# Softmax over 16384 rows: the first two tiles, of 3 and 5 rows, become one tile of 8 rows

## The chip, the core and the metric

One core of a Trainium2 chip runs the whole kernel. The time is device microseconds (us) of one execution; a kernel is given by the median of its runs. Beside it stands the profile of one execution: its span runs from the first to the last instruction of the program.

## The reference

```python
x = np.random.randn(16, 1024, 512).astype(np.float32)

temp = 2.0
x_scaled = x / temp
x_max = np.max(x_scaled, axis=-1, keepdims=True)
exp_x = np.exp(x_scaled - x_max)
return (exp_x / np.sum(exp_x, axis=-1, keepdims=True)).astype(np.float32)
```

A softmax of 16384 rows of 512 float32 values, 33.55 MB in and 33.55 MB out.

## The kernel before

The 16384 rows are 128 rows for each of the 128 partitions of the on-chip memory (SBUF). From here on "a row" is one row per partition: 128 x 512 values, 256 KB. A tile of r rows takes 128 x r neighbouring rows of the input, and partition p holds r of them that lie next to each other in DRAM. So one tile of 15 rows moves as 128 pieces of 30,720 bytes, and the pitch from one partition's piece to the next is 30,720 bytes too.

Ten tiles (`TILES`, L10) cover the 128 rows: 3, 5, and eight of 15. They lie in an arena of 98 rows; the second number of each entry is its place there. The first eight tiles fill the arena. The last two, 8 and 9, are put where the first ones were: `LATE` (L14) says that tile 8 may be loaded when the stores of tiles 0, 1 and 2 have landed, and tile 9 when that of tile 3 has.

The softmax is taken without the maximum. For each row ScalarE (ACT) computes exp(x/2) in place and sums it into `stats` (L204 for the 3 rows of `HEAD`, L271 for groups of five rows). VectorE (DVE) then takes for each group of the list `pairs` one reciprocal of the sums (L166) and one multiplication over all rows of the group (L169). A group never reaches over a tile's end: one group of 3 rows, one of 5, one of 15 for each further tile, and three of 5 rows in the last tile, which is the one where `most` is 1. At the end the sums are tested (L180 to L190); if one were out of bounds, loops further down would compute everything again with the maximum. With this input they do not run.

The order of the work around the change is written out by hand:

- `early()` puts the loads of tile 0 on SP's DMA queue and that of tile 1 on ACT's, ahead of everything else. Tile 0 is loaded in three parts (`SPREAD`): its first row for 126 partitions, the same row for the other two, then rows 1 and 2 for all.
- `loads()` puts tiles 2 to 7 on ACT's queue right after that. Nothing there waits for anything, since these tiles have places of their own in the arena.
- POOL waits until all rows before row 83 (`TURN`) have gone through ACT, then for the stores that `LATE` names, and issues the loads of tiles 8 and 9 (L119, from L179).
- TensorE's queue waits for each tile's load in turn and adds to the semaphore `s_go` the number of groups that ACT may begin (L194). ACT takes one from it before each group.
- SP issues the stores, one for each tile in order, each when the multiplication of the tile's last group is done (`store`, L135).

So the SP queue holds three loads and ten stores, the ACT queue seven loads, and the POOL queue two.

Of the kernel before, what the change touches and what calls it, by code (L numbers as in the profile page):

```python
# [7 lines left out]


TILES = [  # L10
    (3, 0), (5, 3), (15, 8), (15, 23), (15, 38), (15, 53), (15, 68), (15, 83), (15, 0), (15, 15),
]

LATE = {8: (0, 1, 2), 9: (3,)}  # L14
ARENA = 98

HEAD = [3]
E = 5

SPREAD = 0  # L20

TURN = 83

# [5 lines left out]
def kernel(  # L29
# [5 lines left out]
    nc = tc.nc  # L35
# [9 lines left out]
    P = nc.NUM_PARTITIONS  # L45
# [14 lines left out]
    tiles, base = [], 0  # L60
# [5 lines left out]
    def dram(ap, t):  # L66
        b, r, _ = tiles[t]
        return ap[b * P : (b + r) * P].rearrange("(p r) d -> p r d", r=r)

    def sb(t):  # L70
        _, r, at = tiles[t]
        return arena[:, at : at + r, :]
# [5 lines left out]
    owner = [max(t for t, (b, _, _) in enumerate(tiles) if b <= s) for s in starts]  # L78
# [10 lines left out]
    upto = [1 + max(j for j, ks in enumerate(pairs) if owner[ks[0]] == t) for t in range(len(tiles))]  # L89

    ld = [nc.alloc_semaphore(f"ld{t}") for t in range(len(tiles))]
    s_home = {t: nc.alloc_semaphore(f"s_home{t}") for t in LATE}
    s_near = nc.alloc_semaphore("s_near")
    s_end = nc.alloc_semaphore("s_end")
    s_exp = nc.alloc_semaphore("s_exp")
    s_go = nc.alloc_semaphore("s_go")
# [13 lines left out]
    g_rec = nc.alloc_semaphore("g_rec")  # L110
    g_mul = nc.alloc_semaphore("g_mul")

    def load(eng, t):
        r = tiles[t][1]
        parts = [(0, P, 0, r)]
        if t == SPREAD:
            parts = [(0, 126, 0, 1), (126, P, 0, 1), (0, P, 1, r)]
        for p, q, lo, hi in parts:
            eng.dma_start(  # L119
                out=sb(t)[p:q, lo:hi], in_=dram(xf, t)[p:q, lo:hi]  # L120
            ).then_inc(ld[t], 16)

    stored_by = {u: s_home[t] for t, us in LATE.items() for u in us}
    for t, (_, r, at) in enumerate(tiles):
        over = {u for u, (_, ru, au) in enumerate(tiles[:t]) if at < au + ru and au < at + r}
        assert over <= {u for v, us in LATE.items() if v <= t for u in us}

    def landings(ts):
        return 16 * len(list(ts))
# [21 lines left out]
            eng.reg_add(i, i, 1)  # L151

    def early():
        load(nc.sync, 0)
        load(nc.scalar, 1)

    def loads():
        for t in range(2, min(LATE)):
            load(nc.scalar, t)

    def program():
# [14 lines left out]
        nc.gpsimd.wait_ge(s_exp, starts.index(TURN))  # L176
        for t, us in LATE.items():
            nc.gpsimd.wait_ge(s_home[t], landings(us))
# [11 lines left out]
        )._wait_ge(s_tot, 1).then_inc(s_flag, 1)  # L190


        for t in range(len(tiles)):
            nc.tensor.wait_ge(ld[t], 48 if t == SPREAD else 16).then_inc(s_go, owner.count(t))  # L194
        nc.tensor.wait_ge(s_ones, 1)
        nc.tensor.matmul(  # L196
            total[:, :], lhsT=count[:, :], rhs=ones[:, :], start=True, stop=True
# [83 lines left out]
    entry.instructions = []  # L281
    nc.switch_bb("main", None)
    early()
    first = list(entry.instructions)
    at = next(k for k, i in enumerate(head) if type(i).__name__ == "InstDrain")
    entry.instructions = head[:at] + first + head[at:]
    act = []
    entry.instructions = list(entry.instructions) + [i for i in jumps if i not in act]
    nc.switch_body(here, parent=None, valid_engines=[i.engine for i in jumps])
    loads()  # L290
    program()


# [28 lines left out]
```

## Time and profile before

| | |
|---|---|
| median of 4 runs | 160.06 us (160.0 to 160.12) |
| the profiled execution | 160.1 us |
| its span | 158.8 us |
| DVE busy | 73.2 us of the span |
| ACT busy | 80.4 us |
| TensorE, POOL busy | 0.2 and 2.2 us |
| bytes moved | 67.11 MB, 423 GB/s over the span |
| first exponential, first multiplication | begin at 14.85 and 17.04 us |
| stores of tiles 0 and 1 issued | at 18.82 and 22.97 us |
| last store issued | at 135.68 us |

An engine's busy time leaves out the instructions that issue DMAs and wait for semaphores. The DMA share is that of the core's 16 DMA engines, which all queues feed. Every DMA of the kernel that covers all 128 partitions consists of 128 data packets, one for each partition's piece, and 16 small ones of 4 bytes that report the landing. The trace has a record for each packet with its queue, start, duration and bytes; queue q1 is SP's, q10 ACT's, q0 POOL's.

### The profile page before, as it was taken

Reading aid. Unit: us, or ns where it says so; the run is one execution under the profiler, and the core shown is the slowest. Engines: PE = TensorE matmul, PEld = TensorE weight load, DVE = VectorE, ACT = ScalarE, POOL = GpSimd, SP = SyncE. Lnnn points to the kernel's source line nnn. Section 1 sums busy time; section 2 is a strip of 40 time slices with the busy share of each in tenths; the row PEclk is TensorE's granted clock in tenths of the full one; section 3 lists DMA queues with packets and bytes.
Section 4 is the critical chain, followed back from the end, with each engine's and each line's share of the span. In section 5 each row is a group of like instructions: output and inputs, shape, how many; then the busy total and the mean of one; then the engine's idle time right before and its main releaser. Section 6 shows DMA issues by size and latency. Waiting matters only on the chain. (4 is left out here: it accounts for less than half of the span.)

```text
span 158.8 us, 657 instructions
## 1 busy us (share of the span) xinstructions
PE 0.2 (0%) x2; PEld 0.1 (0%) x2; DVE 73.2 (46%) x27; ACT 80.4 (51%) x257; POOL 2.2 (1%) x8
## 2 busy tenths in 40 slices
PE   0000000000000000000000000000000000000000
PEld 0000000000000000000000000000000000000000
DVE  0000470698979913980079300595199199200000
ACT  0302999999990696009920099459800994000000
POOL 0000000000000000000030000000000001000000
DMA  6998999899898989899999999999999999999995
GB/s 215 479 444 381 472 420 416 382 435 493 364 503 387 480 387 480 387 464 402 464 403 464 403 464 402 457 410 449 418 449 418 449 418 441 426 441 426 433 426 255
DMA packets 3024, 67.11 MB, mean 423 GB/s; under 512 B 336, under 2 KB 336, under 8 KB 720
## 3 DMA queue, kind: packets, MB, share of 16 engines
q1 hardware_dynamic: 1728, 34.34, 50.6%
q10 hardware_dynamic: 1008, 24.90, 36.7%
q0 software_dynamic: 288, 7.86, 11.5%
HBM read 33.55 MB, written 33.55 MB: 423 GB/s over the span
## 5 line engine op out<-in xcount | busy, mean ns | idle before, releaser
L271 ACT ACTIVATE arena<-arena x125 | 76.6, 613 | 38.6 <-ACTq L140 38.6
L169 DVE TENSOR_TENSOR arena<-arena,recip 128x7680 f32<-128x7680 f32 (+2 forms) x12 | 70.2, 5847 | 0.4
L166 DVE RECIPROCAL recip<-stats 128x15 f32<-128x15 f32 (+2 forms) x12 | 2.7, 224 | 62.4 <-ACT arena L271 45.5
L271 ACT ACTIVATION_READ_ACCUMULATOR arena<-arena x125 | 23.3, 186 | 0.0
L204 ACT ACTIVATE arena<-arena 128x512 f32<-128x512 f32 x3 | 1.9, 618 | 8.5 <-ACTq L140 8.5
L200 ACT ACT_TABLE_LOAD x1 | 1.3, 1283 | 5.0 <-issue 5.0
L119 POOL DMA_DIRECT2D arena<-in_x_dram x2 | 1.3, 630 | 79.5 <-ACT arena L271 78.4
L180 POOL TENSOR_SCALAR inside<-stats 128x128 f32<-128x128 f32 x1 | 0.6, 629 | 49.6 <-ACT arena L271 49.6
L204 ACT ACTIVATION_READ_ACCUMULATOR arena<-arena 128x1 f32 x3 | 0.6, 186 | 0.0
L196 PE MATMUL total<-ones,count 128*1 128x1 f32 x2 | 0.2, 164 | 135.9 <-DVE inside L184 135.9
L184 DVE SCALAR_TENSOR_TENSOR inside<-inside,stats 128x128 f32<-128x128 f32 x1 | 0.3, 284 | 0.0
L188 DVE TENSOR_SCALAR flag<-total 1x1 int32<-1x1 f32 x1 | 0.1, 147 | 0.3 <-PE total L196 0.3
L196 PEld LDWEIGHTS total<-ones,count 128*1 128x1 f32 x2 | 0.1, 80 | 135.9 <-DVE inside L184 135.9
L175 POOL MEMSET ones<- 128x1 f32 x1 | 0.1, 98 | 1.7 <-POOLq L37 1.7
L306 POOL MEMSET const-float32-0.0<- 128x1 f32 x1 | 0.1, 104 | 0.2 <-issue 0.2
L306 POOL MEMSET const-bfloat16-1.0<- 128x1 bf16 x1 | 0.1, 107 | 0.0
L306 POOL MEMSET const-uint8-127<- 128x1 uint8 x1 | 0.1, 107 | 0.0
L306 POOL MEMSET const-float32-1.0<- 128x1 f32 x1 | 0.1, 104 | 0.0
L184 DVE DVE_READ_ACCUMULATOR inside<-inside,stats 128x1 f32 x1 | 0.1, 83 | 0.0
## 6 DMA issues: line engine op xcount, KB each, us to landing
out_dram<-arena SPq DMA_DIRECT2D x8, 3840.0 KB, 33.3
arena<-in_x_dram ACTq DMA_DIRECT2D x6, 3840.0 KB, 42.1
arena<-in_x_dram POOLq DMA_DIRECT2D x2, 3840.0 KB, 32.2
arena<-in_x_dram ACTq DMA_DIRECT2D x1, 1280.0 KB, 7.0
out_dram<-arena SPq DMA_DIRECT2D x1, 1280.0 KB, 22.8
out_dram<-arena SPq DMA_DIRECT2D x1, 768.0 KB, 14.8
arena<-in_x_dram SPq DMA_DIRECT2D x1, 512.0 KB
arena<-in_x_dram SPq DMA_DIRECT2D x1, 252.0 KB
```

Of the source, the lines that this page charges most:

```text
L119: eng.dma_start(out=sb(t)[p:q, lo:hi], in_=dram(xf, t)[p:q, lo:hi]).then_inc(ld[t], 16)
L166: nc.vector.reciprocal(out=recip[:, b : b + c], in_=stats[:, b : b + c])._wait_ge(s_exp, ks[-1] + 1).then_inc(s_rec, 1)
L169: nc.vector.tensor_mul(out=arena[:, a : a + c], in0=arena[:, a : a + c], in1=recip[:, b : b + c].unsqueeze(2).to_broadcast([P, c, D]),)._w ...
L175: nc.gpsimd.memset(ones[:, :], 1.0).then_inc(s_ones, 1)
L180: nc.gpsimd.tensor_scalar(out=inside[:, :], in0=stats[:, :], scalar1=LO, scalar2=HI, op0=Alu.max, op1=Alu.min,)._wait_ge(s_exp, len(sizes) ...
L184: nc.vector.scalar_tensor_tensor(out=inside[:, :], in0=inside[:, :], scalar=1.0, in1=stats[:, :], op0=Alu.mult, op1=Alu.is_equal, accum_ou ...
L188: nc.vector.tensor_scalar(out=flag[:, :], in0=total[:, :], scalar1=float(N), scalar2=None, op0=Alu.is_ge,)._wait_ge(s_tot, 1).then_inc(s_f ...
L196: nc.tensor.matmul(total[:, :], lhsT=count[:, :], rhs=ones[:, :], start=True, stop=True)._wait_ge(s_cnt, 2).then_inc(s_tot, 1)
L200: nc.scalar.preload_act_table(Exp)
L204: ins = nc.scalar.activation(out=arena[:, b], in_=arena[:, b], func=Exp, scale=0.5, accum_out=stats[:, b : b + 1],)
L271: ins = nc.scalar.activation(out=data, in_=data, func=Exp, scale=0.5, accum_out=stats[:, r : n_rows - E + 1 + r][:, bass.ds(now, 1)],)
L306: nc = _bacc.Bacc("TRN2", target_bir_lowering=False, num_devices=1)
```

## The change

Tiles 0 and 1 become one tile of 8 rows. Its load is still cut at row 3 and comes by the same four DMAs with the same bytes from the same two queues; the parts up to row 3 report to a semaphore of their own, `ld_first`. As the tile's rows are 8 for each partition, partition p now holds the rows 8p to 8p+7 of the first 1024 rows of the input, where it held the rows 3p to 3p+2 of the first 384 and 5p to 5p+4 of the next 640. In DRAM the pitch from one partition's piece to the next is therefore 16,384 bytes in place of 6,144 and 10,240.

ACT's groups stay 3, 5, 5, ... rows. DVE's groups follow the tiles, so the first is one of 8 rows. There is one store of 8 rows in place of two of 3 and 5. All later tiles keep their rows and their places; their numbers fall by one, and `LATE` with them.

```diff
 TILES = [
-    (3, 0), (5, 3), (15, 8), (15, 23), (15, 38), (15, 53), (15, 68), (15, 83), (15, 0), (15, 15),
+    (8, 0), (15, 8), (15, 23), (15, 38), (15, 53), (15, 68), (15, 83), (15, 0), (15, 15),
 ]

-LATE = {8: (0, 1, 2), 9: (3,)}
+LATE = {7: (0, 1), 8: (2,)}
...
-SPREAD = 0
+FIRST = 3
...
+    ld_first = nc.alloc_semaphore("ld_first")
...
-    def load(eng, t):
-        r = tiles[t][1]
-        parts = [(0, P, 0, r)]
-        if t == SPREAD:
-            parts = [(0, 126, 0, 1), (126, P, 0, 1), (0, P, 1, r)]
-        for p, q, lo, hi in parts:
+    def load(eng, t, parts=None):
+        for sem, p, q, lo, hi in parts or [(ld[t], 0, P, 0, tiles[t][1])]:
             eng.dma_start(
                 out=sb(t)[p:q, lo:hi], in_=dram(xf, t)[p:q, lo:hi]
-            ).then_inc(ld[t], 16)
+            ).then_inc(sem, 16)
...
     def early():
-        load(nc.sync, 0)
-        load(nc.scalar, 1)
+        r = tiles[0][1]
+        load(nc.sync, 0, [
+            (ld_first, 0, 126, 0, 1), (ld_first, 126, P, 0, 1), (ld_first, 0, P, 1, FIRST),
+        ])
+        load(nc.scalar, 0, [(ld[0], 0, P, FIRST, r)])

     def loads():
-        for t in range(2, min(LATE)):
+        for t in range(1, min(LATE)):
             load(nc.scalar, t)
...
-        for t in range(len(tiles)):
-            nc.tensor.wait_ge(ld[t], 48 if t == SPREAD else 16).then_inc(s_go, owner.count(t))
+        nc.tensor.wait_ge(ld_first, 48).then_inc(s_go, 1)
+        nc.tensor.wait_ge(ld[0], 16).then_inc(s_go, owner.count(0) - 1)
+        for t in range(1, len(tiles)):
+            nc.tensor.wait_ge(ld[t], 16).then_inc(s_go, owner.count(t))
```

## The prediction

> **What bounds the kernel now.** I read the page's engines and slices first, then the DMA queues, the DMA by stretches, and who waits for whom.
>
> ```profile
> span 158.8 us, 657 instructions
> PE 0.2 (0%) x2; PEld 0.1 (0%) x2; DVE 73.2 (46%) x27; ACT 80.4 (51%) x257; POOL 2.2 (1%) x8
> ...
> DMA  6998999899898989899999999999999999999995
> ...
> DMA packets 3024, 67.11 MB, mean 423 GB/s; under 512 B 336, under 2 KB 336, under 8 KB 720
> ```
>
> No compute engine is busy for more than 51%, while the DMA engines stand at 8 or 9 tenths in every slice but the first and the last. The stretches (length, PE, PEld, DVE, ACT, POOL, clock, DMA share, GB/s) say the same more finely:
>
> ```profile
> 0.00:4.00 4.00, 0.00 (x0) 0.00 (x0) 0.00 (x0) 0.00 (x0) 0.31 (x5) 1.00 0.67 213
> 4.00:24.00 20.00, 0.00 (x0) 0.00 (x0) 4.95 (x4) 10.43 (x31) 0.00 (x0) 1.00 1.02 436
> 24.00:48.00 24.00, 0.00 (x0) 0.00 (x0) 16.95 (x5) 23.53 (x78) 0.00 (x0) 1.00 1.01 431
> 48.00:84.00 36.00, 0.00 (x0) 0.00 (x0) 20.21 (x6) 18.58 (x60) 1.26 (x2) 1.00 1.01 436
> 84.00:124.00 40.00, 0.00 (x0) 0.00 (x0) 21.71 (x5) 19.30 (x63) 0.00 (x0) 1.00 1.00 431
> 124.00:156.00 32.00, 0.19 (x2) 0.09 (x2) 9.39 (x9) 8.57 (x29) 0.63 (x1) 1.00 1.00 430
> ```
>
> From 4 us to 156 us the share is 1.00 to 1.02. Loads alone (4 to 23 us), loads beside stores, and stores alone (124 us on) all run at 430 to 436 GB/s, so it doesn't matter for the end which queue is served when, as long as one has work. The waits of SP's queue and of POOL (engine line, waited for, total us, times, longest):
>
> ```profile
> SPq L137 <- DVE arena L169: 130.3, 10, 20.2
> SPq L257 <- DMA out_dram<-arena: 22.7, 1, 22.7
> ```
> ```profile
> POOL arena L119 <- ACT arena L271: 78.4, 1, 78.4
> POOL arena L119 <- DMA out_dram<-arena: 1.1, 1, 1.1
> ```
>
> The last store is issued at 135.68 us and SP then waits 22.7 us for bytes: a backlog, not a computation. The chain that ended last (DVE 6%, mostly L169) stops at the flag, at 136 us; it isn't the limit. Span = start of the DMAs + all packets + the end.
>
> **The change part by part.** The sum is made for the profiled execution, 158.8 us of span and 1.3 us around it = 160.1 us, 0.04 us above the median; I carry differences over to the median of 160.06.
>
> *The loads at the start.* SP's three DMAs (126x512, 2x512, 128x1024) and ACT's one (128x2560) stay, as do their queues, their order and their bytes. Nothing is moved past them. What is new is the pitch in DRAM, 16,384 bytes for 6,144 and 10,240. No row shows that pitch. The packet records give what the old ones cost: in the first 7 us the packets take, summed and divided by 16 engines, 0.65 us more than a straight line through the sizes (84 ns at 2 KB, 385 ns at 10 KB, 1138 ns at 30 KB, the medians). Bounds: half of the 0.65 us goes (-0.32), or it doubles (+0.65). The nearest rows are ACT's loads: 393 ns median at the pitch of 10,240 and 1141 at 30,720 in the first tiles, 2% and 0.3% above the line; the pitch matters little there. I take 0.
>
> *A rule that speaks against it.* The Trainium skill ("DMA: Bandwidth & Descriptors", Latency and other measured facts) gives copies of 128 pieces of 16 KiB a lower rate where the pitch between partitions is a large power of two: 207 GB/s at 512 KiB and 103 at 4 MiB, against 214. Ours becomes a power of two, but 16 KiB, and it equals the piece, so the store is contiguous. Its mildest figure, 3% of 4.2 MB, would be an estimated 0.3 us; no run here shows it.
>
> *ACT.* Groups stay 3 and 5 rows; the first begins when row 0 to 2 have landed, as now (14.85 us). Cost 0.
>
> *DVE.* Two reciprocals (0.17 and 0.19 us) and two multiplications (128x1536 in 1.76, 128x2560 in 2.82 us) become one of each. The line through 1.76, 2.82 and 8.16 us for 3, 5 and 15 rows gives 4.42 us for 8, the reciprocal 0.21. DVE now begins when ACT has done row 7, at 19.89 us, and ends at 19.89+0.21+4.42+0.06 = 24.58 us, in place of 22.94. Next on it is the first 15-row group, whose reciprocal begins at 29.07 us, after 6.13 us of idling; 4.5 us of this are left. Hidden: 0. Without that cover 1.6 us of DVE would be late.
>
> *The stores.* Those issued at 18.82 and 22.97 us become one at about 24.6 us. What is queued behind it on SP is the 15-row store at 37.5 us, which waits for DVE anyway. The first store's packets began 4.0 us after its issue (22.84 us) and spread to 32.0 us, since each of its 6 KB packets takes turns with a 30 KB load packet; the second's ran from 33.9 to 44.3 us. The new one begins at 24.6+4.0 = 28.6 us; its 8 packets for each engine take turns with 8 load packets, 8 x (611+1138) ns = 14.0 us, so it ends near 42.6 us. (611 ns: the line above at 16,384 bytes.) From 22.8 to 28.6 us ACT's queue alone feeds the engines; its last load ends at 88.6 us, so it can't run dry, and loads alone already run at full rate. Cost of the delay: 0. The next stores come up to 1.7 us earlier, the loads of this phase correspondingly later, by a microsecond at most.
>
> *What waits for those.* POOL's first late load waited for ACT (the 78.4 us row), and may go a microsecond later than 80.72 us; its packets begin at 85.0 us, while ACT's load queue lasts to 88.6 and SP's backlog throughout. The last store is issued at 135.68 us and its first packet leaves at 148.3: 12.6 us of slack against at most 1 us. Cost 0; with that cover gone it would be 1 us.
>
> *What really leaves the path.* Each engine had 8 packets of 234 ns and 8 of 385 ns for the two stores; now it has 8 of 611: 8 x (619-611) = 0.06 us. One 4-byte report packet for each engine, 9 ns, goes too. Together -0.07 us. SP's second issue (0.33 us) and its wait were under the transfers: 0.
>
> *What I can't price exactly.* Between 20 and 48 us, load packets near the begin of these stores ran up to 1387 in place of 1138 ns; summed and divided by 16 engines the excess is 0.22 us, and there is next to none (0.02) from 48 to 86 us. One store fewer may take a share of it away, or a heavier one add to it. Bounds -0.22 and +0.22; I take -0.03, a small share, as the slow packets stand in three bunches (21.6 to 26, 35.8 to 37.4, 45.0 to 46.4 us), and only one store goes.
>
> *A rule for it.* The same page (Bandwidth, Measured) asks for DMAs of at least 1 MiB; its fit of 2.0 us + bytes/436e3 would price 768 KB and 1280 KB at an estimated 3.8 + 5.0 us and the one of 2048 KB at 6.8, 2.0 us less, which would give 158.1. The trace disagrees for this place: the pause between two stores (32.0 to 33.9 us) is filled by load packets at full rate.
>
> Sum: 160.06 - 0.07 - 0.03 = 159.96 us.
>
> **The rivals.**
>
> - *The front gets dearer.* 16 engines read at once, and with the pitch at 16 KB their addresses lie powers of two apart. For: the first 7 us already carry 0.65 us of slow packets, and lost DMA time is lost for good, since no later stage has slack in the DMA. Against: 393 for 385 ns is all that the pitch of 10,240 costs a median packet. If the 0.65 us doubles, 160.06-0.07+0.65 = 160.64 us, slower. It decides from an extra 0.39 us on (0.32 over the median, plus the 0.07 saved).
> - *The disturbances go.* If the 0.22 us between 20 and 48 us belong to the small stores, and half of the front's excess goes: 160.06-0.07-0.22-0.32 = 159.45 us. For: the bunches lie near the stores' issues at 22.97, 37.55 and 46.73 us. Against: the store at 18.82 has none beside its issue, and two of the three bunches belong to stores that stay.
> - *The late store leaves the engines idle.* The first store comes 5.8 us later; were all of it idle, 160.06+5.8 = 165.9 us. Against: ACT's load queue covers it, with 60 us to go.
> - *The change doesn't do what it says.* The order of instructions shows one store of 128x4096 for two and the loads as before; no chance left for this.
>
> **How the numbers follow.** What a measurement of this kernel can tell from no change is about 0.2%, 0.32 us: 159.74 to 160.38. Chances: the forecast 0.62, the dearer front 0.17, the disturbances gone 0.18, idle engines 0.03. Faster 0.19 (a little of the forecast's own spread added), same 0.61, slower 0.20. The forecast's bounds are 160.06-0.07-0.22 = 159.77 and 160.06-0.07+0.22 = 160.21; the range is drawn half-way towards the two rivals, 159.6 to 160.4.
>
> **What would show it.** After: a DMA share of 1.00 in every stretch from 4 to 156 us; 2880 packets (3024 - 144); one store of 2048 KB issued near 24.6 us and landing near 43.5; a multiplication 128x4096 of 4.4 us; the first exponential near 14.85 us; SP's last wait near 22 us; a span of 158.6 to 158.8 us. Wrong if a stretch after 4 us falls below 1.00, if the first exponential comes more than 0.4 us later, or if the packets of 2, 4 and 10 KB take more than 5% over 84, 159 and 393 ns in the median.

## The result and the profile after

The changed kernel takes 160.23 us (median of 35 runs, 159.93 to 160.91), the one before, run beside it, 159.99 us (56 runs). The ratio is 1.0016, 95% interval 1.0010 to 1.0021: slower by 0.24 us, where 0.10 us less was forecast. It is within the 0.2% that was called no change, and inside the range, but the interval excludes both no change and a gain. The profiled execution took 160.21 us.

The page of the changed kernel, its span, engines, slices and DMA:

```profile
span 158.9 us, 654 instructions
PE 0.2 (0%) x2; PEld 0.1 (0%) x2; DVE 72.9 (46%) x25; ACT 80.4 (51%) x257; POOL 2.2 (1%) x8
...
DMA  7999999899989898989898989898989898989895
...
DMA packets 2880, 67.11 MB, mean 422 GB/s; under 512 B 320, under 2 KB 320, under 8 KB 576
...
out_dram<-arena SPq DMA_DIRECT2D x8, 3840.0 KB, 31.0
...
out_dram<-arena SPq DMA_DIRECT2D x1, 2048.0 KB, 19.2
```

The change did what it says: 144 packets fewer and one store of 2048 KB in place of two. The DMA engines are as full as before. The stretches of the changed kernel (same columns as in the prediction):

```profile
0.00:4.00 4.00, 0.00 (x0) 0.00 (x0) 0.00 (x0) 0.00 (x0) 0.31 (x5) 1.00 0.70 210
4.00:24.00 20.00, 0.00 (x0) 0.00 (x0) 3.16 (x2) 9.52 (x28) 0.00 (x0) 1.00 1.01 433
24.00:48.00 24.00, 0.00 (x0) 0.00 (x0) 18.29 (x5) 23.59 (x77) 0.00 (x0) 1.00 1.02 430
48.00:84.00 36.00, 0.00 (x0) 0.00 (x0) 16.82 (x4) 19.33 (x64) 0.00 (x0) 1.00 0.99 427
84.00:124.00 40.00, 0.00 (x0) 0.00 (x0) 22.60 (x6) 18.69 (x62) 1.27 (x2) 1.00 1.02 439
124.00:156.00 32.00, 0.19 (x2) 0.09 (x2) 12.03 (x10) 9.29 (x30) 0.63 (x1) 1.00 1.00 433
```

The share is 0.99 to 1.02 in every stretch after 4 us. A packet counts in the stretch in which it begins, so such a row can be off by a packet for each engine; 0.99 beside 1.02 is that, not idling. But a busy share can't see a packet that takes too long, since a slow packet is busy too. The packet records, set against the straight line through the sizes (8.2 ns + 0.03678 ns for each byte; 611 ns at 16 KB, 1138 ns at 30 KB), summed and divided by 16 engines, in us:

```
                                          before   after
0 to 7 us                                   0.65    0.82
20 to 48 us                                 0.22    0.59
rest                                        0.10    0.09
mean end of the last packet, 16 engines   157.65  157.96
last end of the 16                        158.22  158.33
```

Between 27.4 and 29.2 us, just before and as the first packet of the new store begins (29.39 us), 25 load packets of 30 KB take up to 1742 ns. A DMA has 128 data packets and 16 reports, so eight packets for each engine; the records don't name the engine, and the sixteen last ends are taken as one for each. An engine is then late by what it lost, and the kernel ends with the latest one. All packets together take 0.46 us more for each engine than before (0.53 us of excess, less 0.07 us of packets saved), and until their ends the engines idle for 0.72 us in place of 0.87, so the mean end moved by 0.31 us. The latest end moved by only 0.11, because before one engine ended 0.47 us behind the next anyway. These are single executions; whether the slow packets are also what moves the median is asked of the experiments.

DVE and the waits of SP and POOL after, each from its own view (start, duration; then waiting engine, line, releaser, total us, times, longest):

```profile
20.80 0.20 DVE L167 RECIPROCAL recip<-stats 128x8 f32<-128x8 f32 x1 [20.80 <-ACT arena L274]
21.04 4.42 DVE L170 TENSOR_TENSOR arena<-arena,recip 128x4096 f32<-128x4096 f32 x1
29.99 0.25 DVE L167 RECIPROCAL recip<-stats 128x15 f32<-128x15 f32 x1 [4.52 <-ACT arena L274]
```
```profile
SPq L135 <- DVE arena L170: 134.4, 9, 23.3
SPq L260 <- DMA out_dram<-arena: 19.1, 1, 19.1
```
```profile
POOL arena L117 <- ACT arena L274: 82.1, 1, 82.1
```

The multiplication takes the 4.42 us that the line gave, and DVE still idles 4.52 us behind it. SP's last wait is 19.1 us in place of 22.7, as the last store is issued later (139.43 us). There is still a backlog of stores at the end.

### The profile page after: what moved, and what is told of

It reads as the page before. It is cut to its first block, busy times and chain, and to the rows that moved or that the text cites. A ratio compares the mean times of both kernels' runs of the same rounds, so it can differ in the third digit from the quotient of the medians.

```text
span 158.9 us, 654 instructions
## 1 busy us (share of the span) xinstructions
PE 0.2 (0%) x2; PEld 0.1 (0%) x2; DVE 72.9 (46%) x25; ACT 80.4 (51%) x257; POOL 2.2 (1%) x8
## 2 busy tenths in 40 slices
DMA packets 2880, 67.11 MB, mean 422 GB/s; under 512 B 320, under 2 KB 320, under 8 KB 576
## 6 DMA issues: line engine op xcount, KB each, us to landing
out_dram<-arena SPq DMA_DIRECT2D x1, 2048.0 KB, 19.2
```

## The experiments

Every time is compared with that of the kernel before, run beside it on the same chip. "Excess" is the sum above; "around the first store" means packets that begin from 3.5 us before the first store's first packet to 2.5 us after it.

**Which part of the change costs.** The change moves three things: the rows' layout in DRAM, the moment of the first store (with one multiplication for two), and the join of the stores. C keeps the new layout alone. Its edit to the changed kernel:

```diff
-        most = 1 if t == len(tiles) - 1 else 3
+        most = 1 if t in (0, len(tiles) - 1) else 3
...
     def store(eng, t):
+        if t == 0:
+            for done, lo, hi in ((1, 0, FIRST), (2, FIRST, tiles[0][1])):
+                eng.wait_ge(s_mul, done)
+                eng.dma_start(
+                    out=dram(of, 0)[:, lo:hi], in_=sb(0)[:, lo:hi]
+                ).then_inc(sem_of[0], 16)
+            return
...
-            nc.gpsimd.wait_ge(s_home[t], landings(us))
+            nc.gpsimd.wait_ge(s_home[t], landings(us) + (16 if 0 in us else 0))
```

> The 8-row layout of the changed kernel, but two multiplications (3 and 5 rows) and two stores of them, each issued as soon as its rows are done, as in the kernel before. Layout theory (the 16 KB pitch makes the first loads dearer): stays slower than before, ratio 1.0010 to 1.0020, excess of the packets over the straight line in the first 7 us near 0.8 us. Late-store theory (the first store, 6.7 us later, disturbs the loads more): back at before, ratio 0.9995 to 1.0003, excess between 20 and 48 us near 0.2 us. Big-piece theory (16 KB store packets disturb): also back at before.

Measured: 160.00 us against 160.06, ratio 1.0001 (0.9992 to 1.0011). The excess was 0.79 us in the first 7 us and 0.51 between 20 and 48, the latter not the 0.2 that was expected.

D keeps the old layout, and joins only the multiplication (edit to the kernel before):

```diff
-        if pairs and len(pairs[-1]) < most and owner[pairs[-1][0]] == t:
+        if pairs and len(pairs[-1]) < most and owner[pairs[-1][0]] == t or k == 1:
...
-    upto = [1 + max(j for j, ks in enumerate(pairs) if owner[ks[0]] == t) for t in range(len(tiles))]
+    upto = [1 + max(j for j, ks in enumerate(pairs) if t in [owner[k] for k in ks]) for t in range(len(tiles))]
```

> The layout and loads of the kernel before, but one multiplication over 8 rows, after which both stores are issued, near 25 us. Layout theory: as before, ratio 0.9995 to 1.0003, excess of the first 7 us near 0.65 us. Late-store theory: slower, ratio 1.0010 to 1.0020, with an excess of 0.4 to 0.6 us between 20 and 48 us. Big-piece theory: as before.

Measured: 159.96 us, ratio 0.9997 (0.9988 to 1.0006). Its first store is issued at 24.43 us.

E is the changed kernel with nothing but the store cut again, at the late moment: as C's `store`, with `((1, 0, FIRST), (1, FIRST, tiles[0][1]))`, and `most` as in the changed kernel.

> The changed kernel with its one store cut in two (3 and 5 rows), both issued after the multiplication over 8 rows. Layout theory: as the changed kernel, ratio to before 1.0010 to 1.0020, excess 0.8 us in the first 7 us. Late-store theory: the same ratio, but from 0.4 to 0.6 us between 20 and 48 us. Big-piece theory: as before, 0.9995 to 1.0003.

Measured: 159.90 us, ratio 0.9996 (0.9988 to 1.0005).

> The changed kernel once more, beside the others. All theories: ratio 1.0010 to 1.0021. Layout theory: the excess of the first 7 us is again 0.15 us or more over that of before. Late-store and big-piece theories: the excess between 20 and 48 us is again near 0.6 us, the first 7 us may fall either way.

Measured: 160.29 us, ratio 1.0035 (1.0011 to 1.0058); three of its ten runs took over 160.7 us (160.77, 161.27, 161.89).

So layout and lateness are cleared, and the join of the stores is what costs. That the front's excess went from 0.65 to 0.82 us does not matter either: E has 0.85 there and is not slower, and the changed kernel itself has 0.70 in this second profile. E's stores, from a second profile of it (issue time, then the time to landing):

```profile
25.50 0.84 SPq L137 DMA_DIRECT2D out_dram<-arena  x2
```
```profile
out_dram<-arena SPq DMA_DIRECT2D x1, 1280.0 KB, 28.0
out_dram<-arena SPq DMA_DIRECT2D x1, 768.0 KB, 15.8
```

The two are issued together at 25.50 us, the changed kernel's one at 25.49. Nothing else is edited between the two kernels but that 768 + 1280 KB take the place of 2048 (and that the late load waits for one landing more).

**Packet size, pitch, or moment.** H changes `dram`, so that the first 23 rows of each partition lie together and the 16 KB pieces have a pitch of 46 KB:

```diff
     def dram(ap, t):
         b, r, _ = tiles[t]
+        if t < 2:
+            both = tiles[0][1] + tiles[1][1]
+            return ap[0 : both * P].rearrange("(p r) d -> p r d", r=both)[:, b : b + r]
         return ap[b * P : (b + r) * P].rearrange("(p r) d -> p r d", r=r)
```

> One store of 8 rows as in the changed kernel, but the rows of the first two tiles lie together in DRAM, 23 for each partition: the store's pieces stay 16,384 bytes, their pitch becomes 47,104 bytes, no power of two. Pitch theory (the power of two makes the 16 KB pieces collide): as before, ratio 0.9995 to 1.0003, and no bunch of slow load packets of 0.3 us or more ahead of the first store. Size theory (one first store of large pieces is what disturbs): still 1.0010 to 1.0035, with such a bunch. The loads of these two tiles have the new pitch too, which could change the first 7 us by 0.2 us either way.

Measured: 160.09 us against 160.13, ratio 1.0004 (0.9990 to 1.0017), one of 12 runs at 161.19; excess around the first store 0.39 us. Inconclusive.

Two cuts as in E, with 4 in place of `FIRST`, and with 7:

> The changed kernel with its store cut into two of 4 rows, both after the multiplication over 8 rows: pieces of 8,192 bytes at the pitch of 16,384. Pitch theory: slower than before by some of the 0.16 to 0.35%, as all numbers are powers of two. Size theory: as before, 0.9995 to 1.0003, as with the cut into 3 and 5 rows.

Measured: 159.99 us, ratio 0.9993 (0.9983 to 1.0002), excess around the first store 0.25 us. 8 KB pieces at a pitch of 16 KB cost nothing; the power of two by itself is not it.

> The same, but cut into 7 rows and 1: the first piece has 14,336 bytes, no power of two, but nearly the size of the changed kernel's. Size theory: slower, ratio 1.0010 to 1.0035, with a bunch of slow load packets ahead of the first store. Power-of-two theory: as before. Number-of-stores theory (what counts is that a second small store follows): as before.

Measured: 160.13 us, ratio 1.0006 (0.9997 to 1.0015), excess around the first store 0.64 us. The packets are slow as the size theory has it; the median is that of before, though the interval still reaches the theory's 1.0010.

T is the changed kernel with C's `most`, so that the one store follows two multiplications:

> One store of 8 rows, but after two multiplications of 3 and 5 rows, so issued near 23.5 us and not 25.5. Theories of the store's pieces (size or pitch): as the changed kernel, ratio 1.0010 to 1.0035. If it is the moment of the store (which load tile is then being moved) that matters, the ratio moves: as before, 0.9995 to 1.0003, or a different bunch.

Measured: 160.75 us, ratio 1.0038 (1.0025 to 1.0052), excess around the first store 0.83 us, and another 0.36 between 48 and 86 us, as D, S44 and ONE8 have there too (0.29 to 0.32). Its store of 2048 KB was issued at 23.78 us, so the lateness is no cause: earlier was no better.

**Packet size or bytes of one DMA.** P64 cuts the store by partitions (16 KB pieces, 1 MB each):

```diff
     def store(eng, t):
+        if t == 0:
+            for done, lo, hi in ((1, 0, 64), (1, 64, P)):
+                eng.wait_ge(s_mul, done)
+                eng.dma_start(
+                    out=dram(of, 0)[lo:hi], in_=sb(0)[lo:hi]
+                ).then_inc(sem_of[0], 16)
+            return
...
-            nc.gpsimd.wait_ge(s_home[t], landings(us))
+            nc.gpsimd.wait_ge(s_home[t], landings(us) + (16 if 0 in us else 0))
```

> The changed kernel with its store cut by partitions, 64 and 64: the pieces stay 16,384 bytes, each DMA has 1 MB. Piece theory (the size of the first store's packets makes the bunch of slow load packets): as the changed kernel, ratio 1.0010 to 1.0035, bunch of 0.4 us or more ahead of the first store. Bytes theory (the size of the first DMA makes it): as the cut into 4 and 4 rows, 0.9990 to 1.0003.

ONE8 keeps one DMA of 2 MB and halves its pieces:

```diff
         eng.wait_ge(s_mul, upto[t])
+        if t == 0:
+            b, r, _ = tiles[0]
+            eng.dma_start(
+                out=of[b * P : (b + r) * P].rearrange("(h p r) d -> p h r d", h=2, p=P),
+                in_=sb(0).rearrange("p (h r) d -> p h r d", h=2),
+            ).then_inc(sem_of[0], 16)
+            return
```

> One store of 2 MB, but its pieces are 8,192 bytes, two for each partition; the first 1024 rows of the output land permuted. Piece theory: as the cut into 4 and 4 rows, 0.9990 to 1.0003. Bytes theory: as the changed kernel, 1.0010 to 1.0035.

Measured: P64 160.15 us against 160.15, ratio 1.0004 (0.9995 to 1.0013), with an excess of 0.58 us around its first store, as the changed kernel has. ONE8 160.44 us, ratio 1.0019 (1.0002 to 1.0036), with only 0.15. The medians went with the bytes and the slow packets with the piece size, though the two intervals overlap. Run beside these: the cut into 1 and 7 rows, and X, one store of 23 rows in H's layout (the store of tile 0 dropped, that of tile 1 covering both):

> The changed kernel's store cut into 1 row and 7 rows, both after the multiplication over 8 rows: the first pieces are 2,048 bytes, the second 14,336. First-store theory (only the first store's packet size counts): as the cut into 3 and 5, 0.9990 to 1.0003, and no bunch over 0.3 us. Any-large-piece theory: like the cut into 7 and 1, 1.0003 to 1.0012, with a bunch of 0.4 us or more ahead of the second store.

Measured: 160.20 us, mean 160.45, ratio 1.0019 (1.0002 to 1.0036); 8 runs from 159.92 to 160.35 and 4 from 160.93 to 161.19. No slow packets beside the first store (0.01 us), but 0.65 us of them between 35 and 40 us, ahead of the store of 7 rows. So a small first store doesn't shield the next.

> The layout with the first two tiles' rows together (pitch 47,104 bytes), and one store of all 23 rows after their last multiplication, near 38.5 us; pieces of 47,104 bytes. Piece theory in its simple form (the larger the first piece, the dearer): bunch of 0.6 us or more, ratio 1.0015 or more. If the trouble is particular to pieces of 8 to 16 KB: no such bunch, as the stores of 30 KB show none, 0.9990 to 1.0005.

Measured: 160.92 us, ratio 1.0059 (1.0034 to 1.0085), runs from 160.10 to 162.93; excess around the first store 0.67 us, the longest load packet 2618 ns. SP's waits in it are like before's (22.7 us at the end):

```profile
SPq L145 <- DVE arena L180: 131.4, 8, 35.2
SPq L270 <- DMA out_dram<-arena: 22.8, 1, 22.8
```

The first row's longest wait, 35.2 us, is that for the one first store; the second shows the usual backlog at the end, so this kernel isn't slower for want of ready stores.

**The same three again, beside E.**

> Store cut by partitions, 64 and 64 (16 KB pieces, 1 MB each), once more. Bytes theory: as before again, 0.9990 to 1.0005. Piece theory: 1.0010 or more.

> One store of 2 MB in 8 KB pieces, first 1024 output rows permuted, once more. Bytes theory: slower again, 1.0010 or more. Piece theory: 0.9990 to 1.0003.

> One store of 2 MB, 16 KB pieces at a pitch of 46 KB, once more. Bytes and piece theory both: slower, 1.0010 or more. Pitch theory: as before, 0.9995 to 1.0003.

> The changed kernel with its store cut into 3 and 5 rows, once more. Bytes and piece theory both: as before or a trace faster, 0.9988 to 1.0003. If 0.9996 was chance and the cut doesn't matter, 1.0010 or more as the changed kernel.

Measured, against 160.14 us: P64 160.25, ratio 1.0009 (1.0000 to 1.0018); ONE8 160.18 in the median but 160.31 in the mean, ratio 1.0015 (0.9997 to 1.0032); H 160.53, ratio 1.0030 (1.0015 to 1.0045); E 160.02, ratio 1.0000 (0.9990 to 1.0009). H, unclear at first, is slower here; E again is not. ONE8 and P64 stay unclear, since their intervals hold both no change and the changed kernel's 1.0010.

The spread tells more than the medians. Runs that took over 0.6 us more than the median of before beside them (no run of before itself was above it by more than 0.38; no expectation had named this limit):

```
stores of rows 0 to 7                                runs over 0.6 us
two DMAs of 0.75 + 1.25 or 1 + 1 MB (C D E S44 P64)  0 of 81
1.75 + 0.25 MB (7 and 1 rows)                        0 of 11
one DMA of 2 MB (changed, H, ONE8)                   16 of 93
0.25 + 1.75 MB (1 and 7 rows)                        4 of 12
one DMA of 2 MB, issued 1.7 us earlier (T)           4 of 7
one DMA of 5.75 MB (X)                               8 of 12
```

Where such a run was profiled, the records show what it is: in the 1-and-7 kernel's profile (161.00 us) the sixteen last ends have a mean of 158.03 us, and one engine ends at 159.26. ONE8's first profile (160.64 us) has 157.97 and 158.89, X's (160.59 us) 157.92 and 158.87. In two profiles of E the latest engine is 0.22 and 0.25 us behind the mean. Such a lag stays: in the 1-and-7 kernel's profile the last of a load's sixteen reports comes 0.37 us after their mean at 34.8 us and 1.17 us after it at 64.9 us, and for each of the last five stores 1.25 or 1.26 us after it.

What is shown: the join of the stores costs. E differs in nothing else, and is 0.9996 and 1.0000 of before; the layout (C), the moment and the multiplication (D and E) don't cost.

What in the join costs is not shown. The excess between 20 and 48 us is not enough for it: C, P64 and the 7-and-1 cut have 0.51, 0.57 to 0.61 and 0.64 us there, as the changed kernel has (0.59 and 0.72), and their sixteen ends have means of 157.87 to 157.92 us, yet their ratios are 1.0001 to 1.0009. What is likely, from ONE8, H, X and the 1-and-7 cut against the two small DMAs, is that the bytes in one DMA among the first stores set how often an engine falls behind. The 7-and-1 cut, with 1.75 MB first and 0 of 11, neither fits nor refutes this: at 16 in 93, eleven runs would show none in about one case of eight.

A rival in the order of the transfers can be looked up. The join also moves POOL's first late load, which E issues at 74.08 us and the changed kernel at 84.41. But P64 has it as late as the changed kernel, and ONE8 as early as E (changed kernel, P64, ONE8, the latter two from their second profiles):

```profile
84.41 1.27 POOL L117 DMA_DIRECT2D arena<-in_x_dram  x2 [82.11 <-ACT arena L274]
```
```profile
83.25 1.27 POOL L117 DMA_DIRECT2D arena<-in_x_dram  x2 [80.95 <-ACT arena L281]
```
```profile
75.94 0.73 POOL L117 DMA_DIRECT2D arena<-in_x_dram  x1 [73.64 <-ACT arena L281]
```

P64 had no run over the limit and ONE8 had six of 24, so the runs over the limit don't go with that moment. Why a load packet beside the first store takes 1.7 us, and why more for larger pieces (0.01 to 0.36 us of excess at 6 KB, 0.08 to 0.25 at 8 KB, 0.24 to 0.83 at 14 and 16 KB), no run settles.

## Why the prediction was wrong

- **The bound** was right: all the time is DMA time, the share is full from 4 to 156 us, and the first store could be issued 5.6 to 6.9 us later without cost (D and E).
- **Packets saved, -0.07 us:** 2880 packets, the new ones at 611 ns as worked out. Right, but small against what follows.
- **The step that failed is "What I can't price exactly".** This term, what one heavier store in place of two does to the load packets beside it, was put at -0.03 us with bounds of -0.22 and +0.22. E shows that the join alone makes the difference, so the term measured 0.24 + 0.07 = +0.31 us in the median, of the other sign and beyond the upper bound.
- **Why it was mis-sized:** the forecast tied the slow packets to the moments of issue and gave two of the three bunches to stores that stay. But 0.10 of the 0.22 us stood around the first packet of the first store (22.84 us), one of the two that the change joins. There it became 0.56 us, and 0.71 in the second profile, while the other two bunches went; between 20 and 48 us the sum rose from 0.22 to 0.59 and 0.72 us. The bounds took as a fixed amount what varies from 0.01 to 0.83 us with the first store. But this excess isn't the whole account of the time: 160.06 - 0.07 + 0.37 = 160.36 would overshoot the 160.23, and kernels with as much of it run as before.
- **The other term left out is the latest engine.** "Span = start of the DMAs + all packets + the end" treats sixteen engines as one. The kernel ends with the latest, 0.57 us behind the mean in the profile before, 0.37 after, and 0.9 to 1.2 in three executions of over 160.5 us of other kernels. The forecast reckoned with one execution; the changed kernel's runs reach 160.91 and 161.89 us, before's 160.46 at most. How the measured +0.31 us splits between slow packets and the lag of one engine stays open.
- **The rival "the front gets dearer"** gave the right sign for the wrong reason. The first 7 us rose by 0.17 us in the profile, but C and E have 0.79 and 0.85 there and run as before. The first exponential at 15.77 us (14.85 before) was to refute the forecast; the changed kernel's second profile has it at 14.48, so it varies from execution to execution, and E has it at 15.77 and 16.02 at no cost. The packets of 2, 4 and 10 KB, the other sign, kept their medians (84, 159 and 389 ns).
- **The rule against the change** spoke of pitches. S44, with the changed kernel's pitch in smaller pieces and no slower, and H, with its piece at another pitch and slower in its second set, speak against the pitch as the cause, and E settles it for this kernel. **The rule for it**, by its fit, would have given 2.0 us less; the Trainium skill ("DMA: Bandwidth & Descriptors", Anatomy of one DMA) states this fit for DMAs issued from GpSimd, and these stores are SP's. The trace's objection, that load packets fill the pause, held, and joining even lost 0.24 us.
- **The stores' times** were nearly right: issued at 25.49 us (24.6 forecast, the rest is the later front; 24.21 in the second profile), landing at 25.49 + 19.2 = 44.7 (43.5). "A microsecond at most" for the later loads was mis-sized: POOL's first late load went out at 84.41 us, 3.7 later than before, and the last store at 139.43 us, 3.75 later. The 12.6 us of slack took it.

## What to carry to other kernels

Here, with the DMA engines full throughout, moving the first stores and joining computations was free, and a full busy share hid what was left: compare the packets' durations with the line through their sizes, and the latest engine's end with the mean. While a load stream runs at full rate, try starting the stores with DMAs of about a megabyte rather than one of two or more; here joining them to save packets lost 0.31 us against the 0.07 us that the packets cost. The cut store (E) was 0.9996 and 1.0000 of before, so it repairs the change, but no gain over the kernel before is shown.

## What the runs showed of the hardware

- The whole cost of 144 packets is an estimated 0.07 us, from the line through the sizes and 9 ns for each report; a bunch of some 25 slow load packets, 1.2 to 2.0 us in place of 1.14, takes 0.6 to 0.7 us of each engine on average and leaves no mark in the busy share.
- Kernels that move the same bytes scatter differently: E by 0.8 us (159.69 to 160.51 in 24 runs), X, with one first store of 5.75 MB, by 2.8 us (160.10 to 162.93 in 12).
- The first store's first packet came 3.9 us after its issue (25.49 to 29.39 us), before the change 4.0 us (18.82 to 22.84 us), and 3.4 to 4.8 us in all profiles, in no order by the size of the store (0.25 to 5.75 MB).
